# Two-layer hybrid attention block: the first attention stage takes the projections of its own queries and gate among its heads

## The chip, the core and the metric

The kernel runs on one core of one Trainium2 chip. The metric is the device time of one execution in microseconds (us), median of several runs. One execution was taken by the hardware profiler; its busy times, waits and the time of every instruction are what the text below calls the profile or the trace. The engines are named as in the profile: PE (TensorE matmul) and PEld (its weight load), DVE (VectorE), ACT (ScalarE), POOL (GpSimd), and SP (SyncE), whose queue issues the DMAs. "L685" is line 685 of the kernel.

## What is computed

Two layers (DEPTH = 2) of a mixer block on 512 latent tokens and 256 context tokens of width 1024. All tokens share the weights of a layer. Per layer:

- a modulation vector of 3 x 1024 values from `silu(c) @ w_ada + b_ada`, once for the latent and once for the context tokens: shift, scale and gate;
- `h = rms_norm(x) * (1 + scale) + shift`, for both token sets;
- one projection `h @ w_in` to 3584 columns, split among three head groups. Group A is differential attention: 4 heads, each with two query and key parts of 32 dimensions and one value of 64, so that a head needs two softmaxes and subtracts `lambda` times the second from the first. Group B is grouped-query attention with 6 query heads and 2 key and value heads. Group C is neighbourhood attention with 6 heads and a relative-position bias. Groups A and B have rotary position factors; queries and keys are RMS-normalized per head;
- latent queries attend to their latent keys and all context keys in one softmax; context queries to context keys only, and these only in the first layer, since the output is the latent stream;
- each group's output is multiplied by `silu` of its gate columns, the three are concatenated, multiplied by `w_out` and added to the residual through the modulation gate.

## The kernel before

**Precision.** Matmuls that need fp32 accuracy are made of three: each operand is split into a high part and a low part (`whi`, `wlo` for weights; two `bigL` or `bigC` tiles for `h`), and high x high, high x low and low x high are summed (`mm3`, L682; its three matmuls are L685, L686 and L687). Probabilities, queries, keys and values are split in the same way into two fp16 parts.

**Token tiles.** Tokens come in six tiles of 128: j = 0 to 3 are latent, 4 and 5 context.

**Projection chunks.** The columns of `w_in` are cut into chunks of at most 384 columns (`CH`, L258). For group A these are `a0` (all keys and the values of heads 0 and 1), `a1` (the values of heads 2 and 3, and all queries) and `ga` (the gate, 256 columns). Group B has `b0`, `b1` and `gb`, group C `c0`, `c1`, `c2` and `gn`. `proj` (L715) makes one chunk, token tile by token tile: 24 matmuls into one of two PSUM tiles named `p`, in four steps, after each of which it yields (such a step is called a quantum here), then `evac` (L663). For queries and keys that is a copy and a square on ACT, a sum on DVE, rotary products mostly on POOL (`qk_turn`), a power -1/2 on POOL (`rsqrt`, L156), made for two token tiles at a time, then a product (L504), a cast and a subtraction, and a DMA transpose into place (L540). For gates it is `gate_evac` (L603): tanh on ACT, a product on DVE, for group A a product on POOL (L611), and a write to DRAM (`g_d`); the attention that needs the gate reads it back by `gate_load` (L970).

**Weights.** `WStream` (L53) loads the chunks' weights in pieces of 256 rows and splits each piece: high part by ACT (L82), low part by a subtraction (L85). Six split pieces are kept (`HLB`); each time a piece has served its last token tile, the next is split. The engine of the subtraction goes by the name of the current phase (`VSHARE`, L38): POOL in phases "A" and without a name, DVE in phases "1" and "C", both in turn in "B".

**Attention.** `attn` (L981) walks through units. For group A a unit is one head of one latent token tile (16 units), plus, in layer 0, one head of one context tile (8 units). Per unit of group A:

1. `stage_S`: the scores of the two parts, each into a PSUM tile of 768 columns (two such tiles exist);
2. `stage_M`: the maximum over the row on DVE (L836), the bias of the exponential on ACT (L838);
3. `stage_E`: the exponential on ACT (L850) into a `p32` tile; three of these exist, a unit uses two;
4. `stage_H`, one unit later: the two parts combined on DVE (L866), the fp16 high part on ACT (L870), the low part on POOL (L871), and a DMA transpose into `pt` (L873), of which four exist;
5. `stage_PV`, four units after the scores: the product with the values (L906, L907), and at each fourth unit `pv_evac` with the head norm and the gate (L912 to L935).

**The modulation's rest.** `ada_blocks` (L214) makes one block of 128 modulation columns per step: two loads of 256 KB into two `adw` tiles, 16 matmuls (L236), a copy on DVE (L241), two more matmuls (L243) and a small DVE instruction. `proj` calls it once in every `st["cad"]` token tiles. It takes its PSUM tile from the two named `pv` in phase "1" and from the two named `p` otherwise.

**Order.** The text below is traced into one list of instructions. A scheduler then plays that list through in a simulated time and writes down each engine's order: whatever is ready, the earliest written first. `prio(-400)` lets `stage_S` count as written 400 instructions earlier, `prio(-100)` the loads of a modulation step 100. Each engine then runs its own list strictly in that order, with semaphores between engines. `both` (L1060) writes the units of one group and the quanta of the chunks that fill in (`fill`, L1037) in turn, in proportion; its argument `lead` says how many quanta are written ahead of the first unit. Per layer the text is: chunk `a0` for all tiles (`proj_first`), the chunks of `F1`, attention A with the chunks of `FA`, attention B with those of `FB`, attention C with `FC`, and the output projection.

Of the kernel before, what the change touches and what calls it, by code (L numbers as in the profile page):

```python
# [33 lines left out]


REST = {"C": 7}
AK = [[6, 2, 0, 2], [0, 1, 0, 2]]
VSHARE = {"HA": (0, 1), "H": (0, 1), "G": (1, 1), "T": (1, 4), "HC": (1, 8), "WB": (1, 2), "WC": (1, 1),  # L38
          "W1": (1, 1)}

# [69 lines left out]
def tile_hybrid_block(ctx: ExitStack, tc: tile.TileContext, xT_d, cT_d, ng_d, w_ada, bT_d, w_in, w_out,  # L110
# [7 lines left out]
    V, A, G, PE, SP = nc.vector, nc.scalar, nc.gpsimd, nc.tensor, nc.sync  # L118

    share = Share(nc)  # L120
# [49 lines left out]
    st = {}  # L170
# [82 lines left out]
    def ada_step():  # L253
# [4 lines left out]
    CH = {  # L258
# [4 lines left out]
    }  # L263
    FA = ["b0", "b1", "gb"]
    FB = ["c0", "c1", "c2", "gn"]
    FC = ["y", "o"]
    YE = 2
    F1 = ["a1", "ga"]
    ORDER = [c for c in ["a0"] + F1 + FA + FB + FC if c in CH]
    VCOL = {"a0": (256, 384), "a1": (0, 128), "b0": (128, 256), "c1": (0, 384)}  # L270
    vn = {}

# [11 lines left out]
    for l in range(DEPTH):  # L284
        for c in ORDER:
            cols, n = CH[c]
# [328 lines left out]
    def open_y(l):  # L615
        for k in "hl":
            yT[k] = [big(0, F32R)] + ([big(1, F32R)] if l == 0 else [])
# [411 lines left out]
    def run(gen):  # L1029
        for _ in gen:  # L1030
            pass
# [5 lines left out]
    def fill(l, toks):  # L1037
        for c in toks:
            if c in CH:
                yield from proj(l, [c])  # L1040
            elif c == "y":
                n = 6 if l == 0 else 4
                for j in range(0, n, 2):
                    y_pair(l, j)
                    yield
                    yield
                for j in range(n):
                    if (l, "B", j) not in turned:
                        y_build(l, "gb", j)
                    yield  # L1050
            elif c == "n":
                for db in range(KT):
                    while any((l, "C", j) not in turned for j in range(3)):
                        yield
                    out_head(l, db)
                    yield
            else:
                yield from out_parts(l)

    def both(l, g, chunks, lead=0):  # L1060
        share.phase = g
        f = fill(l, chunks)
        nf = n_quanta(l, chunks)
        na = len(units(l, g)) + 4
        for _ in range(lead):
            next(f, None)
        done = [lead]

        def pump():
            next(f)  # L1070
            done[0] += 1

        st["pump"] = pump
        for x, _ in enumerate(attn(l, g)):
            want = min(nf, lead + (nf - lead - REST.get(g, 0)) * (x + 1) // (na - (YE if g == "B" else 0)))
            while done[0] < want:
                next(f, None)
                done[0] += 1
            if g == "B" and done[0] >= nf and st.get("y") != l:
                run(f)  # L1080
                open_y(l)
                st["y"] = l
        run(f)
# [115 lines left out]
    if True:  # L1199
# [47 lines left out]
        proj_first(0, "a0", [[0, 1, 2, 3, 4, 5]], before0)  # L1247
        for _ in range(AK[0][0] + 1):
            ada_step()
        for l in range(DEPTH):  # L1250
            share.phase = "1"
            st["cad"] = AK[l][1]
            run(fill(l, F1))
            st["cad"] = AK[l][2]
            both(l, "A", FA)
            st["cad"] = AK[l][3]
            both(l, "B", FB)
            while st["done"] < (24 if l == 0 else 32):
                ada_step()
            st["cad"] = 0  # L1260
            both(l, "C", FC + ["n"] * (l + 1 == DEPTH))
            if l + 1 == DEPTH:
                out_tail(l)
                break
            x = [big(0), big(1)]
            open_norm()
            rs = [None, None]
            for db in range(KT):
                out_final(l, db, 1, x[1])
            rs[1] = norm_finish(1)  # L1270
            for db in range(KT):
                out_final(l, db, 0, x[0])
            hT[1] = (big(1, F32R), big(1, F32R))
            for kt in range(KT):
                prio(-800)(build_h)(l + 1, 1, kt, x[1], rs[1])

            def before1(gi, kt):
                if gi == 1:
                    if kt == 0:
                        rs[0] = norm_finish(0)  # L1280
                        hT[0] = (big(0, F32R), big(0, F32R))
                    prio(-800)(build_h)(1, 0, kt, x[0], rs[0])

            proj_first(1, "a0", [[4, 5], [0, 1, 2, 3]], before1)
# [77 lines left out]
```

## Time and profile before

| | |
|---|---|
| median of 3 runs | 934.97 us (934.93 to 936.88) |
| the profiled execution | 930.04 us, span 928.2 us |
| mean granted TensorE clock over the span | 0.95 |
| first score matmul of group A, layer 0 and layer 1 | 107.55 us and 602.99 us from the span's start |
| first gate of `ga` multiplied on POOL (L611), layer 0 | 116.5 us |

The times inside the kernel count from the span's start. In the tables of the trace a row of a group holds the line, engine, operation, output and inputs, shape and count, then the busy time in us and the mean duration in ns, then the idle time of the engine just before these instructions and what ended it. A row of a wait says who waited for whom, us in total, how often, and the longest. A row in order of time begins with start and duration in us. A wait for several semaphores is put down to the one that came last.

### The profile page before, as it was taken

To read this page: it belongs to the slowest core of one execution; us is meant where nothing else is said; L and a number is where in the kernel's file an instruction comes from. 1 tells how busy PE (TensorE), PEld (TensorE's weight loads), DVE (VectorE), ACT (ScalarE), POOL (GpSimd) and SP (SyncE) were. 2 spreads that over 40 slices of the span, in tenths; PEclk is the share of its full clock that TensorE was granted. 3 is DMA by queue.
4 is the path that set the end of the run, shared out by engine and by line. 5 is a ranking of instruction groups with operands and counts; after the bars stand their busy time and mean duration, and the time that the engine had idled before them with its cause. 6 is when DMAs were issued, how large, how long until landed. Compare 5 with 4: busy or idle time off the path is not lost.

```text
span 928.2 us, 17966 instructions
## 1 busy us (share of the span) xinstructions
PE 829.5 (89%) x6386; PEld 709.7 (76%) x6386; DVE 682.7 (74%) x1306; ACT 592.3 (64%) x1269; POOL 541.3 (58%) x502
## 2 busy tenths in 40 slices
PE   5899997997998999797999989989959999988978
PEld 3788886786887889685777889878849888866757
DVE  5975788988678866467765797789877975855853
ACT  5334577885887687476563445478758978757740
POOL 2638846998798465432441047939988776732420
PEclk9899999998999999899999999999979999987979
DMA  9925895644979997989898713884556889995642
GB/s 307 331 90 135 204 215 133 154 85 127 194 156 221 195 221 170 227 213 229 183 234 235 243 61 101 184 189 101 140 132 156 168 188 249 240 253 134 134 114 83
DMA packets 361449, 165.47 MB, mean 178 GB/s; under 512 B 256656, under 2 KB 355216, under 8 KB 361104
## 3 DMA queue, kind: packets, MB, share of 16 engines
q1 hardware_dynamic: 361360, 164.33, 73.9%
q8 instruction: 50, 0.82, 0.4%
q14 instruction: 39, 0.32, 0.1%
HBM read 86.55 MB, written 15.47 MB: 110 GB/s over the span
## 4 chain that ended last, share of the span: by engine, by line
PE 46%; DVE 15%; DMA 13%; POOL 9%; issue 8%; ACT 7%; SPq 1%; DVEq 0%; POOLq 0%; ACTq 0%
PE proj L685 7%; PE proj L687 7%; PE proj L686 6%; PE sc L781 5%; DMA pt<-hl 4%; PE pv L906 3%; PE op L1093 3%; PE op L1094 3%; PE op L1095 2%; ACT p L850 2%; DVE mx L836 2%; DMA raw<-in_w_in_dram 2%; DMA stB<-in_btab_dram 2%; POOL hl L871 2%; POOL wlo L85 1%
## 5 line engine op out<-in xcount | busy, mean ns | idle before, releaser
L871 POOL TENSOR_TENSOR hl<-p,hl 128x768 f16<-128x768 f32 (+3 forms) x138 | 204.2, 1484 | 179.7 <-ACT hl L870 139.7
L685 PE MATMUL proj<-whi,bigL 128*128 128x384 f32 (+1 forms) x592 | 203.4, 344 | 9.8 <-DVE tb L608 3.8
L686 PE MATMUL proj<-wlo,bigL 128*128 128x384 f32 (+1 forms) x592 | 200.3, 338 | 0.9 <-POOL wlo L85 0.7
L687 PE MATMUL proj<-whi,bigL 128*128 128x384 f32 (+1 forms) x592 | 197.7, 336 | 0.0
L850 ACT ACTIVATE p<-sc,nb,gsc 128x768 f32<-128x768 f32 (+3 forms) x200 | 166.0, 844 | 14.3 <-DVE p L866 5.0
L836 DVE TENSOR_REDUCE mx<-sc 128x1 f32<-128x768 f32 (+2 forms) x128 | 118.7, 931 | 31.7 <-PE sc L781 31.2
L685 PEld LDWEIGHTS proj<-whi,bigL 128*128 128x128 f32 x592 | 115.4, 195 | 19.9 <-DVE tb L608 5.4
L870 ACT CAST hl<-p 128x768 f16<-128x768 f32 (+3 forms) x144 | 103.7, 725 | 33.0 <-DMA pt<-hl 18.5
L686 PEld LDWEIGHTS proj<-wlo,bigL 128*128 128x128 f32 x592 | 115.5, 195 | 3.9 <-POOL wlo L85 1.6
L687 PEld LDWEIGHTS proj<-whi,bigL 128*128 128x128 f32 x592 | 114.4, 194 | 3.3 <-issue 2.4
L85 POOL TENSOR_TENSOR wlo<-raw,whi 128x768 fp32r<-128x768 f32 (+1 forms) x44 | 82.9, 1893 | 30.0 <-ACT whi L82 24.8
L82 ACT CAST whi<-raw 128x768 fp32r<-128x768 f32 (+1 forms) x104 | 80.3, 779 | 30.8 <-DMA raw<-in_w_in_dram 16.2
L906 PEld LDWEIGHTS <-pt 128*128 128x128 f16 x736 | 65.9, 99 | 41.2 <-DMA pt<-hl 25.7
L85 DVE TENSOR_TENSOR wlo<-raw,whi 128x768 fp32r<-128x768 f32 (+1 forms) x60 | 65.2, 1090 | 25.3 <-ACT whi L82 22.5
L685 PE MATMUL proj<-whi,bigC 128*128 128x384 f32 (+2 forms) x224 | 75.8, 339 | 0.8 <-ACT xn L468 0.8
L686 PE MATMUL proj<-wlo,bigC 128*128 128x384 f32 (+2 forms) x224 | 74.8, 334 | 0.0
L687 PE MATMUL proj<-whi,bigC 128*128 128x384 f32 (+2 forms) x224 | 74.6, 335 | 0.0
L156 POOL TENSOR_TENSOR rsqb<-rsqb,half 128x12 f32<-128x12 f32 (+2 forms) x25 | 68.2, 2726 | 10.5 <-DVE rsqb L155 8.4
L907 PEld LDWEIGHTS <-pt 128*128 128x128 f16 x736 | 66.6, 100 | 4.2 <-issue 1.2
L906 PE MATMUL pv<-vA,pt 128*128 128x128 f16 (+2 forms) x424 | 52.2, 229 | 13.6 <-DMA pt<-hl 13.0
L838 ACT ACTIVATE nb<-mx,lnp,gsc 128x1 f32<-128x1 f32 (+1 forms) x104 | 39.6, 385 | 37.6 <-DVE mx L836 26.5
L781 PE MATMUL sc<-bigL 128*128 128x512 f16 (+4 forms) x184 | 46.1, 310 | 17.3 <-ACT p L850 16.7
(320 smaller groups left out, 2042.2 us busy)
## 6 DMA issues: line engine op xcount, KB each, us to landing
raw<-in_w_in_dram SPq DMA_DIRECT2D x56, 384.0 KB, 4.1
adw<-in_w_ada_dram SPq DMA_DIRECT2D x68, 256.0 KB, 3.8
raw<-in_w_in_dram SPq DMA_DIRECT2D x24, 256.0 KB, 3.6
raw<-in_w_out_dram SPq DMA_DIRECT2D x16, 384.0 KB, 4.0
g_d<-tb SPq DMA_DIRECT2D x20, 192.0 KB, 2.6
gt<-g_d SPq DMA_DIRECT2D x18, 192.0 KB, 2.9
hl<-in_w_ada_dram SPq DMA_DIRECT2D x12, 256.0 KB, 5.0
pt<-in_w_ada_dram SPq DMA_DIRECT2D x12, 256.0 KB, 5.2
```

The lines of the kernel that those rows point to most:

```text
L82: self.nc.scalar.copy(out=hi, in_=raw2)
L85: self.share("W").tensor_tensor(out=lo, in0=raw2, in1=hi.bitcast(F32), op=ALU.subtract)
L156: G.tensor_tensor(out=y, in0=x, in1=half[:, 0:n], op=ALU.pow)
L685: PE.matmul(ps, lhsT=xh, rhs=hi, start=(kt == 0), stop=False)
L686: PE.matmul(ps, lhsT=xh, rhs=lo, start=False, stop=False)
L687: PE.matmul(ps, lhsT=xl, rhs=hi, start=False, stop=(kt == KT - 1))
L781: PE.matmul(ps, lhsT=q, rhs=k, start=n == 0, stop=n == b[2] - 1)
L836: V.tensor_reduce(out=mx[:, 0:ns], in_=ps[:, 0:w * ns].rearrange("p (a b) -> p a b", b=w), axis=AX.X, op=ALU.max)
L850: A.activation(out=p[:, w * x:w * x + w], in_=u["ps", i][:, w * x:w * x + w], func=AF.Exp, bias=u["nb", i][:, x:x + 1], scale=lc[l]["sc"][ ...
L870: A.copy(out=hl[:, 0:n], in_=p)
L871: lo_eng.tensor_tensor(out=hl[:, n:2 * n], in0=p, in1=hl[:, 0:n], op=ALU.subtract)
L906: PE.matmul(po[r, :], lhsT=pt[:, b, r], rhs=V_[:, vt, c0:129], start=first, stop=False)
```

## The change

`F1` is gone: `a1` and `ga` are now the first two chunks of `FA`, so they are written among the units of attention A, not ahead of them. `both` is called for group A with `lead` = 9: nine quanta, which is two finished token tiles of `a1` and the beginning of the third, are written ahead of the first unit. After unit x the text has reached 9 + (n - 9)(x + 1) / m quanta, rounded down, with n = 120 and m = 28 in layer 0 and n = 96 and m = 20 in layer 1. The order in which weights are loaded (`ORDER`) stays what it was.

Phase "1" is no longer set inside the loop over the layers; it now holds only from the first `proj_first` to the first attention A. The first attention A and the chunks in it all run under the name "A", with what hangs on the name: the engine of the weights' low part and the PSUM tile of the modulation steps.

The cadence of modulation steps (`AK`) has three numbers a layer now. The first, 6, is as before. In layer 0 there is one step per 5 token tiles over the 30 tiles of attention A (before: one per 2 over the 12 tiles of `F1`, none in attention A). In layer 1 there is one per 2 over 24 tiles (before: one per tile over the 10 tiles of `F1`, none in attention A). Stage B keeps one per 2.

```diff
-AK = [[6, 2, 0, 2], [0, 1, 0, 2]]
+AK = [[6, 5, 2], [0, 2, 2]]
...
-    FA = ["b0", "b1", "gb"]
+    FA = ["a1", "ga", "b0", "b1", "gb"]
     FB = ["c0", "c1", "c2", "gn"]
     FC = ["y", "o"]
     YE = 2
-    F1 = ["a1", "ga"]
-    ORDER = [c for c in ["a0"] + F1 + FA + FB + FC if c in CH]
+    LEAD = {"A": 9}
+    ORDER = [c for c in ["a0"] + FA + FB + FC if c in CH]
...
         for l in range(DEPTH):
-            share.phase = "1"
             st["cad"] = AK[l][1]
-            run(fill(l, F1))
+            both(l, "A", FA, LEAD["A"])
             st["cad"] = AK[l][2]
-            both(l, "A", FA)
-            st["cad"] = AK[l][3]
             both(l, "B", FB)
```

## Prediction

> **What bounds the kernel now.** I read the head of the page first, then the busy time by stretch, then the waits of PE inside those stretches, then the instructions around the first scores.
>
> ```profile
> span 928.2 us, 17966 instructions
> PE 829.5 (89%) x6386; PEld 709.7 (76%) x6386; DVE 682.7 (74%) x1306; ACT 592.3 (64%) x1269; POOL 541.3 (58%) x502
> ```
>
> The profiled execution took 930.04 us with a span of 928.2 us; the median of the timed runs, 934.97 us, lies 4.93 us above it. PE is idle for 928.2 - 829.5 = 98.7 us in all, so no reordering is worth more than that, and the change touches only the two first attention stages. The busy times by stretch show these (columns: stretch, its length, busy time and instructions of PE, PEld, DVE, ACT and POOL, granted clock, DMA share, GB/s). The first three rows are layer 0: projections alone, then attention A early and late. The last three are layer 1, in the same order.
>
> ```profile
> 70.00:107.00 37.00, 35.66 (x264) 30.64 (x264) 22.44 (x62) 15.97 (x41) 32.93 (x34) 0.95 0.63 141
> 107.00:150.00 43.00, 36.90 (x344) 30.66 (x345) 36.13 (x71) 32.58 (x82) 20.03 (x18) 0.96 0.97 228
> 150.00:226.00 76.00, 65.51 (x450) 58.56 (x448) 67.61 (x93) 55.20 (x131) 72.84 (x73) 0.93 0.53 119
> 570.00:603.00 33.00, 32.25 (x292) 29.43 (x290) 23.35 (x60) 16.21 (x41) 31.61 (x33) 1.00 0.76 177
> 603.00:630.00 27.00, 23.22 (x197) 20.09 (x198) 22.38 (x48) 21.57 (x55) 11.79 (x17) 1.00 0.80 182
> 630.00:695.00 65.00, 51.47 (x359) 44.81 (x356) 56.51 (x78) 46.53 (x109) 60.49 (x57) 0.89 0.53 124
> ```
>
> Three things are to be seen. Before the first scores (70 to 107, 570 to 603) PE is 96 to 98% busy and POOL 89 to 96%. In the first part of attention (107 to 150, 603 to 630) no engine is full: DVE is highest in layer 0 with 36.13/43 = 84%, PE in layer 1 with 86%, and POOL is below half. After that POOL is nearly full: 72.84/76 = 96% in layer 0, 60.49/65 = 93% in layer 1, while PE loses 10.5 and 13.5 us. So the stage first leaves POOL empty and is later bound by it.
>
> What PE waits for in the early part (first two rows: 108 to 160; next three: 598 to 640) and in the full part of layer 1 (last two: 640 to 695):
>
> ```profile
> PE sc L781 <- ACT p L850: 4.9, 4, 2.6
> PE ada L236 <- DMA adw<-in_w_ada_dram: 1.4, 2, 0.9
> ...
> PE sc L781 <- ACT p L850: 2.2, 2, 1.5
> PE ada L236 <- DMA adw<-in_w_ada_dram: 1.2, 2, 1.0
> ...
> PE sc L781 <- ACT p L850: 6.3, 3, 3.9
> PE pv L906 <- DMA pt<-hl: 4.9, 3, 3.1
> ```
>
> A score waits until the exponential has read its PSUM tile, and that sits at the end of maximum (DVE), exponential (ACT) and subtraction (POOL): only three `p32` tiles exist and a unit uses two. PE is held up by this ring of engines, not by lack of matmuls.
>
> **Part 1, the head start of two query tiles.** The new text lets attention begin after 9 quanta, two projected query tiles, where the old one puts 12 tiles (layer 1: 10) ahead of it. But the written order is only a priority, and scores already carry a lead of 400 places. The first scores stand here: first row of the DMA issues, then the turned context keys, the turned first query tile, DVE's weight splits and PE's projection at that moment, and the first score of layer 0 and of layer 1.
>
> ```profile
> DMA to landing us min/median/max: 3.1/3.8/6.2
> 97.99 5.11 SPq L540 DMA_TRANSPOSE bigC<-stg  x2
> 103.78 1.23 SPq L540 DMA_TRANSPOSE bigL<-stg  x1
> 103.34 2.06 DVE L85 TENSOR_TENSOR wlo<-raw,whi 128x512 fp32r<-128x512 f32 x2
> 105.45 1.10 DVE L85 TENSOR_TENSOR wlo<-raw,whi 128x512 fp32r<-128x512 f32 x1
> 107.13 0.28 PE L685 MATMUL proj<-whi,bigL 128*128 128x256 f32 x1
> 107.55 0.39 PE L781 MATMUL sc<-bigL 128*128 128x512 f16 x1
> 602.99 0.39 PE L781 MATMUL sc<-bigL 128*128 128x512 f16 x1 [0.41 <-DMA bigL<-stg]
> ```
>
> 103.78 plus a landing of 3.8 is 107.58, so the score of layer 0 ran as soon as its query had landed, and layer 1 waited 0.41 us for the same transfer. Neither waited for the ten later tiles. What lies ahead of those transposes (rotary and power steps of `a0` on the 89% busy POOL) is written before the changed place in both texts, and until then PE has nothing but `a1` and `ga` to project. I take 0. At best the three DVE splits that stand at 103.34 to 106.55 and now leave DVE let it come 3.2 us sooner; a loss would need a longer chain ahead of it, which the new text does not write.
>
> **Part 2, the order after the first scores.** The projection at 107.13 is 256 wide, so the six `a1` tiles are through and `ga` has begun: some 7 of the 12 tiles, 28 quanta, in the new text too. Now comes the difference: in the old text all gate tiles stand ahead of every maximum, exponential and subtraction of attention; in the new one 9 + 111(x + 1)/28 quanta stand ahead of what follows unit x, 28 for x = 4, so the units 0 to 4 stand ahead of the tiles still open, which fill in behind. No instruction is added. The attention units can run further ahead while POOL is empty, and then POOL has less left when it is full. What that is worth I bound by POOL's own work, at the rate that it reached when full (0.958 in layer 0, 0.931 in layer 1), with the splits of part 3 added (11.65 and 12.9 us):
>
> - layer 0, 107 to 226: (20.03 + 72.84 + 11.65) / 0.958 = 109.1 us where it took 119: 9.9 us.
> - layer 1, 603 to 695: (11.79 + 60.49 + 12.9) / 0.931 = 91.5 us where it took 92: 0.5 us.
>
> PE does not forbid it: 36.90 + 65.51 = 102.4 us of its 119. So the bounds are 0 and -10.4 us. I take half, **-5.2 us**: the ring of three `p32` tiles keeps units from running freely ahead, and the waits for it (4.9 and 2.2 us in the early part) are of the size of that half.
>
> **Part 3, eight weight splits a layer.** The phase name decides who subtracts: DVE in phase "1", POOL in phase "A". Six weight pieces are kept ready, so the last tile of `a1` frees four places (last two pieces of `ga`, first two of `b0`) and that of `ga` four more (last two of `b0`, first two of `b1`): 6 pieces of 512 columns and 2 of 768. Layer 0, then layer 1 (in whose seven DVE splits one of `a0`'s time is counted too):
>
> ```profile
> L85 DVE TENSOR_TENSOR wlo<-raw,whi 128x512 fp32r<-128x512 f32 x6 | 6.5, 1092 | 0.6 <-ACT wlo L278 0.6
> L85 DVE TENSOR_TENSOR wlo<-raw,whi 128x768 fp32r<-128x768 f32 x2 | 1.9, 952 | 0.8 <-ACT whi L82 0.8
> L85 POOL TENSOR_TENSOR wlo<-raw,whi 128x768 fp32r<-128x768 f32 x12 | 23.1, 1942 | 5.1 <-ACT wlo L278 2.8 <-ACT whi L82 2.3
> L85 DVE TENSOR_TENSOR wlo<-raw,whi 128x512 fp32r<-128x512 f32 x7 | 5.0, 716 | 0.9 <-ACT whi L82 0.5 <-ACT wlo L278 0.5
> L85 DVE TENSOR_TENSOR wlo<-raw,whi 128x768 fp32r<-128x768 f32 x2 | 2.8, 1394 | 0.0
> L85 POOL TENSOR_TENSOR wlo<-raw,whi 128x768 fp32r<-128x768 f32 x10 | 21.4, 2152 | 1.2 <-ACT whi L82 1.2
> ```
>
> DVE gets rid of 8.4 us and of 6 x 0.716 + 2.8 = 7.1 us. POOL has no 512-wide split here; two thirds of the wide one gives 6 x 1.29 + 2 x 1.94 = 11.65 us and 6 x 1.43 + 2 x 2.15 = 12.9 us. They are already inside the sums of part 2, so **0** here. What hides them is POOL's idle time of 43.0 - 20.0 = 23.0 and 27.0 - 11.8 = 15.2 us right after the first scores; without that cover they cost their full 24.5 us, and the matmuls that need `wlo` are late next. But who holds up whom is also to be seen:
>
> ```profile
> 156.54 1.65 POOL L871 TENSOR_TENSOR hl<-p,hl 128x768 f16<-128x768 f32 x1
> 156.90 1.45 DVE L504 TENSOR_TENSOR xn<-xn,rsq 128x128 f32<-128x128 f32 x1
> 158.37 1.63 POOL L871 TENSOR_TENSOR hl<-p,hl 128x768 f16<-128x768 f32 x1
> 158.53 1.62 DVE L504 TENSOR_TENSOR xn<-xn,rsq 128x128 f32<-128x128 f32 x1
> ```
>
> A DVE product of 128 columns takes 1.45 and 1.62 us and ends about when POOL's subtraction ends, though it started after it. So a microsecond moved to POOL can come back as a blocked microsecond on DVE: at worst 24.5 - 15.5 = 9.0 us. I keep that as a rival. [...]
>
> **Part 4, the modulation steps.** Old cadence 2 in the first projections, none in attention A; new cadence 5 (layer 0) and 2 (layer 1) over all of the stage. The number of steps until stage B is the same, 6 in layer 0; in layer 1 the list runs out in both. But outside phase "1" a step takes its PSUM tile from the two that the projections use: its first matmul may wait for one on PE, with scores and projections queued behind, and the next projection waits while the step holds it. Where that is already so, in the stage with attention B, and where the moved ones stand now (16 matmuls a step: 7, 6 and 7 steps):
>
> ```profile
> L236 PE MATMUL ada<-adw,cS x112: 272/273/298, 266.4 to 360.8; 128*32 128x128 f32 x112
> L236 PE MATMUL ada<-adw,cS x96: 269/273/298, 108.9 to 254.6; 128*32 128x128 f32 x96
> L236 PE MATMUL ada<-adw,cS x112: 272/273/298, 572.4 to 609.2; 128*32 128x128 f32 x112
> PE proj L685 <- DVE gnk L322: 2.0, 1, 2.0
> PE ada L243 <- DVE vnc L545: 1.5, 1, 1.5
> ```
>
> The last two rows are all the waits of PE in 262 to 365 that a missing PSUM tile can explain: 3.5 us for 7 steps, 0.5 us each. 13 moved steps make 6.5 us without cover and nothing where scores stand ready; I take half, **+3.25**. Their loads, two of 256 KB a step on SP's queue, move with them and no longer arrive late: the waits for `adw` above, 1.4 + 1.2, go: **-2.6**. Gate writes and gate loads move along on the same queue; a gate is needed first at the fourth unit's end, and its tile is projected before the scores begin, so 0.
>
> **Sum.** -5.2 + 0 + 3.25 - 2.6 = -4.55 us: the profiled execution would go from 930.04 to 925.5, the median from 934.97 to **930.4 us**.
>
> **Rivals.**
> - *It changes nothing.* Part 1 says that the stage was interleaved already. Against it: the priority of the units among the gate tiles does change. 935.0.
> - *Attention runs fully ahead.* All of part 2, the late loads gone, the steps covered: -10.4 - 2.6 = -13.0, so 922.0. Against it speaks the ring of three `p32` tiles.
> - *POOL is full (slower).* In layer 1 POOL has (31.61 + 11.79 + 60.49) of 125 us, 83%, and from 630 on it is the bound. If the eight splits land behind 630, all 12.9 us lie on the path; layer 0, with 23 us of cover, stays at 0: 947.9. It decides as soon as POOL's idle time after the first score of layer 1 falls below 12.9 of its 15.2 us.
> - *POOL's splits hold DVE (slower).* The 9.0 us of part 3 on an 84 to 89% busy DVE: 944.0. For it: the four rows. Against it: maxima, DVE's largest group, read PSUM and are not held.
> - *The two PSUM tiles (slower).* Part 2 brings nothing, and 6.5 us stand uncovered against 2.6 saved: 938.9.
>
> **Chances.** Forecast 0.36, own range 926 to 933; fully ahead 0.12; nothing 0.15; POOL full 0.17; DVE held 0.08; PSUM tiles 0.12. A measurement here can tell about 0.2%, 1.9 us, from no change. Faster is 0.36 + 0.12 = 0.48, same 0.15, slower 0.37. The range from 919 to 948 takes in all cases with their spread and leaves out less than 2 in 10 at its ends.
>
> **What would show it.** Part 1: the first scores within 3 us of 107.5 and, by the same distance, of 603. Part 2: POOL's busy time between the first score and 43 us later rises well above 20.0 us, more than the moved splits make, and the subtractions of attention come at shorter distance there. Part 3: eight splits a layer change from DVE to POOL; wrong if PE waits for `wlo` or if DVE's two-input operations get longer. Part 4: waits of a projection that begin while a modulation step holds a tile. The forecast fails if POOL is the bound from the first score on, or if attention A of layer 1 (92 us from 603 to 695) lengthens.

## The result, and the profile after

The changed kernel takes **944.23 us** (median of 8 runs, 939.18 to 948.27) where the kernel before took 934.95 us beside it (8 runs, 931.68 to 938.5): a ratio of **1.0098, 95% interval 1.007 to 1.0126**. It is 1% slower. The forecast was 930.4 us.

The profiled execution of the changed kernel took 948.27 us, 4 above its median; that of the kernel before lay 5 below. Their spans therefore differ by 18.3 us where the medians differ by 9.3. What a view shows of the difference is a matter of its kind and place, not of the last microsecond.

The head of the page of the changed kernel:

```profile
span 946.5 us, 17940 instructions
...
PE 833.4 (88%) x6386; PEld 718.2 (76%) x6386; DVE 671.2 (71%) x1290; ACT 591.0 (62%) x1269; POOL 568.9 (60%) x518
```

PE is idle for 946.5 - 833.4 = 113.1 us where it was idle for 98.7: 14.4 of the 18.3 us. PE itself is busy 3.9 us longer, with the same 6386 matmuls. DVE's work fell by 11.5 us and POOL's rose by 27.6 us.

The busy times by stretch of the changed kernel, in the columns of the prediction: from the first score of layer 0 on, and from that of layer 1 on, early and late.

```profile
111.50:155.00 43.50, 37.58 (x321) 34.29 (x324) 30.82 (x56) 32.38 (x83) 29.42 (x27) 0.92 0.75 173
155.00:230.00 75.00, 65.60 (x478) 57.76 (x471) 64.92 (x100) 54.03 (x130) 71.75 (x69) 0.95 0.58 136
...
603.50:630.00 26.50, 22.36 (x182) 19.19 (x183) 18.44 (x33) 19.44 (x49) 20.63 (x19) 0.87 0.82 179
630.00:695.00 65.00, 52.95 (x417) 47.23 (x416) 48.26 (x86) 45.55 (x111) 48.56 (x55) 0.89 0.59 137
```

POOL does more in the stretch that it left empty before (29.42 us after the first score of layer 0, where it was 20.03; 20.63 in layer 1, where it was 11.79). But this is not attention running ahead. The same stretches for the subtractions of attention alone (L871; columns: stretch, length, busy time and instructions of DVE and POOL, clock, DMA share, GB/s), two rows of the kernel before and two of the changed one, and then for the weight splits alone (L85) in the changed kernel:

```profile
107.00:150.00 43.00, 0.00 (x0) 7.38 (x5) 0.96 0.97 228
603.00:630.00 27.00, 0.00 (x0) 4.97 (x3) 1.00 0.80 182
...
111.50:155.00 43.50, 0.00 (x0) 8.31 (x5) 0.92 0.75 173
603.50:630.00 26.50, 0.00 (x0) 3.29 (x2) 0.87 0.82 179
```

```profile
111.50:155.00 43.50, 0.00 (x0) 8.72 (x6) 0.92 0.75 173
603.50:630.00 26.50, 0.00 (x0) 9.12 (x7) 0.87 0.82 179
```

The number of subtractions stays at five in layer 0 and falls from three to two in layer 1. The moved splits are what fills POOL there. Afterwards POOL is as full as before in layer 0 (71.75 of 75 us) and no longer full in layer 1 (48.56 of 65 us, where it was 60.49). Yet PE loses 12 us of those 65, about as much as before (13.5): there POOL is not the bound any more, and PE stands as long as it did.

What it stands for is told by the waits of PE over the whole span (who waited for whom, us in total, times, longest). First the kernel before, then the changed one:

```profile
PE sc L781 <- ACT p L850: 18.9, 16, 3.9
PE pv L906 <- DMA pt<-hl: 18.8, 19, 3.1
...
PE ada L236 <- DMA adw<-in_w_ada_dram: 4.8, 6, 2.0
...
PE ada L243 <- DVE adt L241: 2.1, 2, 1.7
```

```profile
PE sc L781 <- ACT p L850: 19.2, 17, 3.1
PE pv L906 <- DMA pt<-hl: 15.7, 16, 2.7
PE proj L685 <- DVE mG L249: 9.6, 5, 3.2
...
PE ada L243 <- DVE adt L241: 5.9, 8, 1.8
...
PE ada L236 <- DMA adw<-in_w_ada_dram: 2.8, 2, 2.1
...
PE ada L236 <- DVE vA L592: 2.5, 1, 2.5
...
PE proj L685 <- DVE mA L246: 1.7, 2, 0.9
```

`L246` and `L249` are the last DVE instruction of a modulation step: when it is done, the step gives its PSUM tile back. A projection that waits for it waits for a tile named `p`. These waits and those inside a step (L243) make 9.6 + 5.9 + 1.7 = 17.2 us, where they made 2.1. That is 15.1 us more. A step also waits for a tile itself, until DVE or ACT has read a projection out of it: 2.5 us above, 1.3 for L468 and 0.9 for L608, 4.7 us where there was none. The waits for the ring of attention (`p`, `pt`) are only 2.8 us smaller, and those for late loads 2.0.

These waits belong to the list: `e10_lead17` below has nearly the same list for PE, and in its profiled execution, whose span is 10.3 us shorter, they make 7.8 + 6.0 + 1.9 = 15.7 us in place of the 17.2. But they are not the loss one for one. Of the 14.4 us that PE idles longer, 4.0 lie ahead of the first score of layer 0 (19.7 us, where it was 15.7), where next to none of these waits stands.

One of these waits as it happens, right after the first scores of layer 0: PE in order of time (start, duration), then DVE in the same microseconds.

```profile
103.24 0.43 PE L236 MATMUL ada<-adw,cS 128*32 128x128 f32 x8 [0.70 <-DMA adw<-in_w_ada_dram]
...
110.36 0.42 PE L236 MATMUL ada<-adw,cS 128*32 128x128 f32 x8
...
112.17 0.28 PE L243 MATMUL ada<-sel,adt 128*128 128x2 f32 x2
115.45 0.39 PE L685 MATMUL proj<-whi,bigL 128*128 128x256 f32 x1 [3.00 <-DVE mG L249]
```

```profile
111.52 1.76 DVE L512 TENSOR_TENSOR stg<-xn,stg 128x512 f16<-128x512 f32 x1 [0.38 <-ACT stg L511]
113.20 0.94 DVE L836 TENSOR_REDUCE mx<-sc 128x1 f32<-128x768 f32 x1
...
114.33 0.94 DVE L836 TENSOR_REDUCE mx<-sc 128x1 f32<-128x768 f32 x1
115.19 0.20 DVE L249 TENSOR_SCALAR mG<-ada,bT 128x2 f32<-128x2 f32 x1
```

And POOL beside the first of these:

```profile
111.46 1.27 POOL L85 TENSOR_TENSOR wlo<-raw,whi 128x512 fp32r<-128x512 f32 x1
```

The step takes its tile with its first eight products at 103.24 and has the second eight at 110.36 and the last two at 112.17, 0.43 + 0.42 + 0.28 = 1.13 us of PE time. It keeps the tile until 115.39, 12.15 us. Its last instruction, 0.20 us long, stands in DVE's list behind the subtraction that makes the low part of queries and two score maxima. That subtraction takes 1.76 us here, where one of the same shape at 102.77 took 0.89, with two POOL products of 0.46 and 0.90 us beside it; here a moved weight split of 1.27 us runs on POOL beside it, so part 3 may have a share in this wait, though one row does not show it. All that while one of the two projection tiles is gone, and PE, with the next projection first in its list, ends by doing nothing for 3.00 us. Paired in this way, the 20 steps up to attention B of the two layers hold a tile for 6.5 us each on average in the changed kernel (the first six of them still one named `pv`). In the kernel before it is 7.1 us, leaving aside one step of 29.8 us that begins at 543.50, while layer 0 ends.

### The profile page after: what moved, and what is told of

Read it like the earlier page. It is cut to its first block, busy times and chain, and to the rows that moved or that the text cites. A ratio compares the mean times of both kernels' runs of the same rounds, so it can differ in the third digit from the quotient of the medians.

```text
span 946.5 us, 17940 instructions
## 1 busy us (share of the span) xinstructions
PE 833.4 (88%) x6386; PEld 718.2 (76%) x6386; DVE 671.2 (71%) x1290; ACT 591.0 (62%) x1269; POOL 568.9 (60%) x518
## 5 line engine op out<-in xcount | busy, mean ns | idle before, releaser
L871 POOL TENSOR_TENSOR hl<-p,hl 128x768 f16<-128x768 f32 (+3 forms) x138 | 209.5, 1522 | 173.4 <-ACT hl L870 155.2
L685 PE MATMUL proj<-whi,bigL 128*128 128x384 f32 (+1 forms) x592 | 208.9, 353 | 22.4 <-DVE mG L249 8.8
L686 PE MATMUL proj<-wlo,bigL 128*128 128x384 f32 (+1 forms) x592 | 203.5, 344 | 1.8 <-DVE wlo L85 1.2
L687 PE MATMUL proj<-whi,bigL 128*128 128x384 f32 (+1 forms) x592 | 202.6, 344 | 0.0
L836 DVE TENSOR_REDUCE mx<-sc 128x1 f32<-128x768 f32 (+2 forms) x128 | 119.2, 932 | 38.9 <-PE sc L781 35.9
L685 PEld LDWEIGHTS proj<-whi,bigL 128*128 128x128 f32 x592 | 119.7, 202 | 32.2 <-DVE mG L249 9.6
L85 POOL TENSOR_TENSOR wlo<-raw,whi 128x768 fp32r<-128x768 f32 (+1 forms) x60 | 104.5, 1747 | 38.6 <-ACT whi L82 33.4
L686 PEld LDWEIGHTS proj<-wlo,bigL 128*128 128x128 f32 x592 | 119.9, 203 | 4.3 <-DVE wlo L85 1.5
L687 PEld LDWEIGHTS proj<-whi,bigL 128*128 128x128 f32 x592 | 119.1, 202 | 3.0 <-issue 1.0
L82 ACT CAST whi<-raw 128x768 fp32r<-128x768 f32 (+1 forms) x104 | 80.2, 778 | 37.7 <-DMA raw<-in_w_in_dram 17.1
L906 PEld LDWEIGHTS <-pt 128*128 128x128 f16 x736 | 65.7, 99 | 35.2 <-DMA pt<-hl 20.5
L838 ACT ACTIVATE nb<-mx,lnp,gsc 128x1 f32<-128x1 f32 (+1 forms) x104 | 39.5, 384 | 26.1 <-DVE mx L836 19.7
L85 DVE TENSOR_TENSOR wlo<-raw,whi 128x768 fp32r<-128x768 f32 (+1 forms) x44 | 47.6, 1086 | 11.0 <-ACT whi L82 10.2
```

Source lines behind the costliest of these rows:

```text
L82: self.nc.scalar.copy(out=hi, in_=raw2)
L85: self.share("W").tensor_tensor(out=lo, in0=raw2, in1=hi.bitcast(F32), op=ALU.subtract)
L685: PE.matmul(ps, lhsT=xh, rhs=hi, start=(kt == 0), stop=False)
L686: PE.matmul(ps, lhsT=xh, rhs=lo, start=False, stop=False)
L687: PE.matmul(ps, lhsT=xl, rhs=hi, start=False, stop=(kt == KT - 1))
L836: V.tensor_reduce(out=mx[:, 0:ns], in_=ps[:, 0:w * ns].rearrange("p (a b) -> p a b", b=w), axis=AX.X, op=ALU.max)
```

## The experiments

Each ratio is to the kernel before on the same chip, with its 95% interval. "Order" is the new text of the stage, "splits" the eight weight splits a layer on POOL, "steps" the modulation steps with their cadence and PSUM tile.

### One part of the change undone

`e1_ada_psv`: the changed kernel, with the steps of attention A in the tiles named `pv`.

```diff
-ps = (psV if share.phase == "1" else psP).tile(..., tag="pv" if share.phase == "1" else "p", ...)
+ps = (psV if share.phase in ("1", "A") else psP).tile(..., tag="pv" if share.phase in ("1", "A") else "p", ...)
```

> The changed kernel, but the modulation steps inside attention A take their PSUM tile from the two named pv again. Theory PSUM (a modulation step holds one of the two tiles of the projections; the waits of PE for it and around it sum to about 16 us in the changed kernel's trace): most of the loss goes, ratio to the kernel before 0.998 to 1.004, and the waits of a projection for the step's last DVE instruction (L249, L246) disappear. Theory splits (eight weight splits a layer on POOL) and theory order (attention written ahead of the projections costs by itself): 1.007 to 1.012.

Measured 937.82 us, 1.0024 (0.9997 to 1.0052), as the theory of the tile had it: its trace has only 0.5 + 1.1 us of the waits that made 17.2. `e2_splits_dve`: the changed kernel, with the eight splits a layer back on DVE.

```diff
-self.share("W").tensor_tensor(out=lo, ...)
+eng = self.nc.vector if i in self.vset else self.share("W")
+eng.tensor_tensor(out=lo, ...)
...
+W.vset = {i for l in range(DEPTH) for i in pidx[l, "ga"][2:] + pidx[l, "b0"] + pidx[l, "b1"][:2]}
```

> The changed kernel, but the eight weight splits a layer that went to POOL are on DVE again, named piece by piece; the modulation steps stay as changed. Theory splits: ratio to the kernel before 0.998 to 1.003. Theories PSUM and order: 1.006 to 1.012, the 16 us of waits around the modulation steps still there.

Measured 957.05 us, 1.0232 (1.0186 to 1.0278): without the move to POOL the changed kernel is 1.3% slower still, which no theory had. `e3_order_only`: the new order alone, with the splits on DVE as in e2, the tiles as in e1, and the steps where they were (one per 2 tiles of `a1` and `ga` in layer 0, one per tile in layer 1).

```diff
-AK = [[6, 5, 2], [0, 2, 2]]
+AK = [[6, 0, 2], [0, 0, 2]]
...
-if st["cad"] and st["n"] % st["cad"] == 0:
+cad = (2, 1)[l] if c in ("a1", "ga") else st["cad"]
+if cad and st["n"] % cad == 0:
```

> The changed order of the text alone: a1 and ga among the units after nine quanta, but the modulation steps as before (one per two tiles of a1 and ga, one per tile in layer 1, PSUM tiles named pv) and the eight splits on DVE. Theory order: ratio to the kernel before 1.007 or more. Theories PSUM and splits: 0.993 to 1.002, below 1 by as much as the order itself is worth (the forecast's part 2 was 5.2 us, 0.6%).

Measured 940.48 us, 1.0053 (1.0021 to 1.0085): the order alone loses half a per cent, between the ranges of the theories. `e6_lead25` and `e10_lead17`: the changed kernel with another head start.

```diff
-LEAD = {"A": 9}
+LEAD = {"A": 25}
```

> The changed kernel with a lead of 25 quanta instead of 9: the whole of a1 is written ahead of the first unit, ga and the rest among the units. Theory order: the loss shrinks to half or less, ratio to the kernel before 1.000 to 1.005. Theories PSUM and splits: unchanged, 1.007 to 1.012, since the steps still fall into attention A and take the projections' tiles and the splits stay on POOL.

> The changed kernel with a lead of 17 quanta, four query tiles instead of two. The planner gives almost the same orders as with 9 (14 lines of PE's 7575 differ). Theory lead (how many tiles are written ahead matters): below 1.007. Theory that the written lead is ignored because the first scores wait for keys and query anyway: 1.007 to 1.013, as the changed kernel.

Measured 946.06 us, 1.0116 (1.0064 to 1.0169), and 943.35 us, 1.0075 (1.0042 to 1.0108). Both intervals overlap that of the change. With 17 the scheduler writes nearly the list of 9 for PE (14 lines of difference among 7575), so that run shows mostly that the result repeats. The head start is not what costs.

### One part alone on the kernel before

`e4_before_ada`: no step in the first projections, one per 3 (layer 0) and 2 (layer 1) tiles in attention A, in the tiles `p`.

```diff
-AK = [[6, 2, 0, 2], [0, 1, 0, 2]]
+AK = [[6, 0, 3, 2], [0, 0, 2, 2]]
```

> The kernel before with part 4 alone: no modulation step in the first projections; in attention A one per 3 tiles (layer 0, 6 steps) and one per 2 (layer 1, 7 steps), which then take one of the two PSUM tiles of the projections. Order and splits as before. Theory PSUM (with the pv tiles the changed kernel fell from 1.0098 to 1.0024): 1.004 to 1.010. Theory that the modulation steps cost only in the new order: 0.998 to 1.002.

Measured **921.59 us, 0.9851 (0.982 to 0.9882)**: it beats both kernels, and neither theory had that. `e5_before_splits`: the eight splits a layer on POOL (the edit of e2 with GpSimd for VectorE).

> The kernel before with part 3 alone: the eight weight splits a layer after a1 and ga are made by POOL, all else as before. By the forecast's rival of a full POOL: 1.005 to 1.014. By the second experiment (in the changed kernel the same splits on DVE made it 1.3% slower): no loss, 0.992 to 1.002, and if below 0.998 a version faster than both.

Measured 948.45 us, 1.0138 (1.0109 to 1.0166). `e8_before_psp`: the steps of the first projections keep their place, but take a tile `p`.

```diff
-ps = (psV if share.phase == "1" else psP).tile(...)
+pool_, tag_ = (psV, "pv") if st["done"] <= 6 else (psP, "p")
+ps = pool_.tile([128, 512], F32, tag=tag_, name="ada")
```

> The kernel before, order, cadence and splits untouched; only the PSUM tile of the modulation steps in the first projections changes from pv to p. Theory PSUM in its strict form (the tile alone, wherever the step stands): 1.004 to 1.010, with waits of a projection for the step's last DVE instruction. If it needs attention beside it (DVE busy with maxima, so that the step holds its tile longer): 0.999 to 1.003.

Measured 950.95 us, 1.0164 (1.0139 to 1.0189), more than the strict form of the theory allowed. `e9_order_pool`: the new order with the splits on POOL, the steps as before in place and tile (e3 without the edit of e2). This is the change without part 4.

> The changed order with the modulation steps as before (among a1 and ga, PSUM tiles pv) and the eight splits on POOL as in the changed kernel. Against the third experiment (the same with the splits on DVE, 1.0053) it prices the splits; against the first (1.0024, the steps spread, pv) the cadence. Theory PSUM with splits on POOL harmless: 0.995 to 1.003. Theory order (the written order costs by itself): 1.004 or more.

Measured **930.23 us, 0.9938 (0.9915 to 0.9961)**. Parts 1 to 3 together gain 0.6%, and what turns the change into a loss is the modulation steps: 1.0098 - 0.9938 = 1.6%, some 15 us. `e11_late_steps`: as e9, but no step in `a1` and `ga` and then the cadence and tiles of e4.

> The changed order and the splits on POOL, with the modulation steps placed as in the fourth experiment: none while a1 and ga are projected, then one per 3 tiles (layer 0) and one per 2 (layer 1), PSUM tiles p. Theory PSUM: 1.005 or more, as the changed kernel, since the steps take the projections' tiles. Theory place (what matters is that no step falls between the first tiles, where keys and queries are made ready): 0.982 to 0.995. Theory plan scatter (each new plan moves by about 1% either way, whatever part is changed): anything from 0.985 to 1.016, no help.

Measured 957.44 us, 1.0223 (1.0176 to 1.027). The same placing that gained 1.5% in the old order is 2.2% slower than before in the new one.

So single parts do not add up. The splits on POOL cost 1.4% in the old order (e5) and gain 1.15% (e9 against e3) and 1.3% (the change against e2) in the new one. The new order loses 0.5% with the splits on DVE (e3) and gains 2.0% with them on POOL (e9 against e5).

### Do parts have a price at all?

Every edit makes the scheduler write the whole list anew, so I changed the list without changing any work: the lead of the scores 300 instead of 400.

```diff
-@prio(-400)
+@prio(-300)
```

> The kernel before with one number of the planner changed: scores count as written 300 instructions earlier instead of 400. No work, engine, tile or step changes, but the planned orders do (6342 lines of PE's). Theory plan scatter: off 1 by 0.4% or more, either way. Theories that explain the times by parts (PSUM, splits, order): 0.997 to 1.003.

> The changed kernel with the same number at 300. Theory plan scatter: off 1.0098 by 0.4% or more, either way. Theories by parts: 1.007 to 1.013.

Measured 941.65 us, 1.0054 (1.0026 to 1.0082), for the kernel before and 947.18 us, 1.0096 (1.0062 to 1.0129), for the changed one. An edit without work moves the first by 0.5% and leaves the second where it was. I then repeated four variants with this lead.

> The kernel before with the modulation steps of the first projections moved into attention A (fastest so far, 0.985 of the kernel before), and the scores' lead in the planner set from 400 to 300. Theory of parts (the moved steps save time by themselves): 1.0054 (the kernel before at 300) less the same 1.5%, so 0.990 +- 0.003, about 927 us. Theory of the redrawn plan (what a part is worth depends on the whole order): the saving differs by at least 0.5% from 1.5%, so below 0.985 or above 0.9955.

> The changed kernel with the modulation steps of attention A in the tiles named pv, and the scores' lead at 300. Theory of parts (the two projection tiles cost the changed kernel 0.7%): 0.7% below the changed kernel at 300 (1.0096), so 1.002 +- 0.003, about 938 us. Theory of the redrawn plan: a difference other than 0.7% by 0.5% or more, so below 0.9975 or above 1.0075.

> The changed kernel's order and its splits on POOL with the modulation steps as before (0.994 at 400), and the scores' lead at 300. Theory of parts: the modulation's part costs the changed kernel the same 1.6% at 300, so 1.0096 - 0.016 = 0.994 +- 0.003, about 930 us. Theory of the redrawn plan: off by 0.5% or more from that, below 0.989 or above 0.999.

> The kernel before with the eight splits a layer on POOL (1.0138 at 400), and the scores' lead at 300. Theory of parts: 1.0054 + 0.0138 = 1.019 +- 0.003, about 954 us. Theory of the redrawn plan: off by 0.5% or more from that, most likely below 1.014.

e14 (e4 with 300): 921.51 us, 0.9852 (0.9813 to 0.9891). Here the scheduler wrote the very same list as with 400, so it is a second measurement of e4 and tells the theories not apart. e15 (e1 with 300): 948.44 us, 1.0141 (1.0103 to 1.018), not 1.002: the gain from the tiles `pv` has become a loss. e16 (e9 with 300): 923.79 us, 0.9877 (0.9832 to 0.9921): part 4 costs 1.0096 - 0.9877 = 2.2% here, some 20 us. e17 (e5 with 300): 948.14 us, 1.0127 (1.0088 to 1.0165), 0.7% above e12 and not 1.4%. With the changed lead these lists part from the others only in attention B of layer 0, so the two leads are not two independent draws.

Part 4 has two halves, the place of the steps and their tile. Two last runs fill the square: the edit of `e9_order_pool` with the tiles `p` of the change, at both leads.

> The changed kernel with the modulation steps where they were before (one per 2 tiles of a1 and ga in layer 0, one per tile in layer 1, none else in attention A), in the tiles named p as in the change. It fills the fourth place of a square: steps as before in pv 0.994, spread in pv 1.002, spread in p 1.010. Theory of the place (spreading the steps over the stage is what costs): as with pv, 0.994 to 0.998, about 932 us. Theory of the tile (the two projection tiles are what costs): at least 0.7% above the pv version, 1.001 or more, about 938 us or more.

> The same with the scores' lead in the planner at 300. The other three places of the square there: steps as before in pv 0.988, spread in pv 1.014, spread in p 1.010. Theory of the place: 0.985 to 0.995, about 927 us. Theory of the tile: 1.000 or more. If the two leads disagree on which theory holds, neither place nor tile has a price of its own.

Measured 963.86 us, 1.0288 (1.0253 to 1.0323), and 959.15 us, 1.0269 (1.0225 to 1.0312).

| steps, lead | tiles `pv` | tiles `p` |
|---|---|---|
| as before, 400 | 0.9938 (e9) | 1.0288 (e18) |
| spread over attention A, 400 | 1.0024 (e1) | 1.0098 (the change) |
| as before, 300 | 0.9877 (e16) | 1.0269 (e19) |
| spread over attention A, 300 | 1.0141 (e15) | 1.0096 (e13) |

Neither half has one price. For steps that stand close together beside the projections the tiles `p` cost 3.5 and 3.9%, and 1.6% in the old order (e8). For spread steps the tiles make +0.7 and -0.45%. Spreading costs 0.9 and 2.6% in `pv` and saves 1.9 and 1.7% in `p`. Nor do the waits of PE around the steps decide by themselves: e13 has 9.2 + 4.2 + 1.6 us of those that made 17.2 in the change, e15 only 2.9 + 0.4, and e15 is not the faster one. The change leaves the one corner that is fast at both leads.

The heads of the pages of e9 and e18, in this order:

```profile
span 928.6 us, 17958 instructions
...
PE 825.8 (89%) x6386; PEld 708.8 (76%) x6386; DVE 652.6 (70%) x1290; ACT 589.6 (63%) x1269; POOL 565.9 (61%) x518
```

```profile
span 962.2 us, 17933 instructions
...
PE 838.9 (87%) x6386; PEld 716.9 (75%) x6386; DVE 676.3 (70%) x1290; ACT 588.9 (61%) x1269; POOL 560.6 (58%) x518
```

PE's idle time is 102.8 and 123.3 us. e18 against e9 differs only in the tile of the steps: 33.6 us of span, of which 20.5 are idle and 13.1 are matmuls that took longer. Projections wait only 2.9 + 0.4 us for a step's tile in e18. The larger waits stand inside the steps, for their DVE copy and their loads, and were 0.4 and 2.3 us in e9:

```profile
PE ada L243 <- DVE adt L241: 11.3, 10, 3.6
PE ada L236 <- DMA adw<-in_w_ada_dram: 10.8, 9, 2.2
```

So the tile's high price here is measured, but the held tile is not shown to be the way in which it is paid.

Where the change loses 3.00 us, e9 has two steps under way beside the first scores. PE in order of time:

```profile
104.28 0.42 PE L236 MATMUL ada<-adw,cS 128*32 128x128 f32 x8
...
108.19 0.43 PE L236 MATMUL ada<-adw,cS 128*32 128x128 f32 x8
...
109.33 0.39 PE L781 MATMUL sc<-bigL 128*128 128x512 f16 x1 [0.27 <-DMA bigL<-stg]
...
110.38 0.43 PE L236 MATMUL ada<-adw,cS 128*32 128x128 f32 x8 [0.23 <-DMA adw<-in_w_ada_dram]
...
112.28 0.36 PE L687 MATMUL proj<-whi,bigL 128*128 128x256 f32 x1
```

The first step, too, lasts from 104.28 until its last DVE instruction ends at 113.55, 9.3 us, and the second begins meanwhile. But they hold tiles `pv`, which nobody else wants before the first product with the values (129.3 us), and the projections run on behind them.

Last, the waits of PE in e4 and in e9:

```profile
PE pv L906 <- DMA pt<-hl: 10.7, 13, 2.5
PE sc L781 <- ACT p L850: 10.5, 8, 4.1
...
PE ada L243 <- DVE adt L241: 6.2, 5, 2.3
...
PE proj L685 <- DVE mG L249: 4.9, 4, 2.4
...
PE proj L685 <- DVE mB L249: 2.2, 1, 2.2
```

```profile
PE sc L781 <- ACT p L850: 31.2, 19, 4.0
PE pv L906 <- DMA pt<-hl: 18.9, 19, 2.1
```

e4 has waits of the change's kind, 6.2 + 4.9 + 2.2 = 13.3 us. But its waits for the ring fell from 18.9 + 18.8 = 37.7 to 21.2 us, by more than that. In the change the ring gave back 2.8 us for 15.1. In e9 no row of a projection or a step that waits in this way is longer than 0.6 us, and the ring's waits are the largest of the four kernels. A wait of PE for one thing often takes the place of a wait for another; what an edit costs is the balance, and the list of a single kind does not show it.

## Why the prediction was wrong, point by point

**The step that failed is part 4 of the sum**, "+3.25" for the PSUM tiles and "-2.6" for the loads, +0.65 us together. The runs put 1.6% in its place, some 15 us (the change against e9), and 2.2%, some 20 us, at the other lead. The loads did come in time (4.8 to 2.8 us of waiting, 2.0 of the 2.6). The price of a step was mis-sized. I took it, 0.5 us, from the stage with attention B, where seven steps cost 3.5 us, and halved it. A step holds its tile 6.5 us for 1.1 us of work, since its DVE instructions, and at times its second load, stand in strict lists behind others. The waits for steps and inside them are 15.1 us longer than before in place of at most 6.5, and steps wait 4.7 us more for a tile. The time a step holds its tile could be read in the trace of before (7.1 us); I priced the wait by another stage and did not ask for it. Rival "the two PSUM tiles" named this mechanism and the side, at 938.9 us; its bound of 6.5 us was too small by more than half. That part 4 makes the loss is shown by e9 and e16; that these waits are the way in which it does is argued, since e15 is rid of them and no faster than e13.

**Part 2 and the sum of parts 1 to 3.** The forecast was -5.2 us. e9 is these three parts and measured 930.23 against 935.94 us beside it, -5.7 (0.9938). That the sum came out is luck. At the other lead the same parts make -12.5 us (e16, 923.79 against 936.32). The mechanism of part 2 did not appear: by its own mark POOL's busy time should have risen by more than the moved splits make, and the splits make 8.72 of the 9.4 us in layer 0 and all of the 8.8 us in layer 1, with no more subtractions of attention than before; e9 too has five and three of them in the 43 and 27 us after its first scores. Rival "attention runs fully ahead" falls with that. Nor did the terms hold: part 3 was priced at 0 and alone costs 1.4% (e5), part 2 alone costs 0.5% (e3). They are worth something only together. Their prices were read from one schedule, as if it stayed when the next part was added.

**Part 1.** The first score of layer 1 came at 603.51, within 3 us of the forecast. In layer 0 it came at 111.51, 4.0 late, which by my own mark counts against me. But e13, whose lists are the same up to attention B, has it at 107.70. Between 71.8 and 78.6 us the changed kernel's clock was 0.50 and e13's 1.00 (columns as above; the changed kernel first):

```profile
71.80:78.60 6.80, 6.12 (x25) 5.74 (x26) 3.36 (x9) 3.32 (x11) 6.80 (x8) 0.50 0.36 110
```

```profile
71.80:78.60 6.80, 6.80 (x58) 6.00 (x51) 4.38 (x20) 2.42 (x8) 6.80 (x7) 1.00 0.37 112
```

So the delay belongs to this execution and not to the change; the head start is worth nothing, as forecast, and e6 and e10 agree (first scores at 110.48 and 108.93).

**Part 3.** The splits moved as said. L85 goes from 44 to 60 instructions on POOL, 82.9 to 104.5 us, and from 60 to 44 on DVE, 65.2 to 47.6 us. Sixteen splits changed engine: 21.6 us more on POOL (forecast 24.5), 17.6 less on DVE (forecast 15.5). The cover held: POOL was 29.42 of 43.5 us busy after the first score of layer 0. Rival "POOL is full" falls with the 48.56 of 65 us in layer 1, since seven of the eight splits of that layer ran ahead of 630 us, and with e2, which takes the load off POOL and is slower. In the old order e5 lost 1.4%, as this rival had it there; what it lost by is not examined. Rival "POOL's splits hold DVE" falls as a price of 9.0 us, though not as a mechanism. Of the twelve products of the shape that I had shown being held, those over 0.7 us, seven before and four after, each began while a POOL subtraction ran (L85 or L871) and ended about 0.15 us behind it; the others took 0.28 to 0.68 us. On average the twelve take 786 ns where they took 1160, and all products of L504 together take 60.5 us where they took 66.9; the subtractions of L512, one of which is the row of 1.76 us above, take 18.7 us where they took 16.5. In sum that is 79.2 us where it was 83.4, so in sum these operations were not held longer. The maxima of L836 were not held, as I had said: none of the 128 took more than 0.96 us in either kernel.

**My marks for failure.** "The forecast fails if attention A of layer 1 lengthens": from the first score to the first score of attention B it went from 120.7 to 131.4 us. Before, then after, in the columns of the stretches:

```profile
603.00:723.70 120.70, 102.69 (x746) 90.89 (x746) 101.15 (x156) 92.69 (x217) 95.72 (x94) 0.94 0.60 143
```

```profile
603.50:734.90 131.40, 108.48 (x796) 95.34 (x797) 95.93 (x154) 90.61 (x215) 104.38 (x102) 0.88 0.64 148
```

PE is busy 5.8 us longer in it, with 50 more matmuls and a mean clock of 0.88 instead of 0.94, and idle 4.9 us longer. The mark came true, but it proves less than I thought. The changed kernel comes to this stage with some 120 matmuls fewer behind it (4145 where it was 4265), so a part of the length is work that the kernel before had done by then; and e9, which is faster than the kernel before, takes 123.1 us for it.

**What stays open.** Why the same steps gain 1.5% in the old order (e4) and lose in the new one (e11) is told only as a balance of waits, not derived. The square rests on two leads that share the first third of the list. An edit without work moved single variants by -0.6% (e9 to e16) to +1.2% (e1 to e15), so differences below that, such as the 0.7% of e1 against the change, are not the price of anything. The 3.5 and 3.9% of the tile of dense steps lie well above that scatter. The 1.6 and 2.2% of part 4 lie above any single shift, but a difference holds two of them, so that it rests on both leads having the same sign.

## What to carry to other kernels

Before a step with a small PSUM need is moved, ask whose tile it takes and how long it holds it: not its PE time, but the time until its last reader has run on an engine with a strict list, and who wants that tile meanwhile. Where a scheduler writes the whole order anew, a change of several parts has no sum of prices: run the parts alone and together, and first measure what an edit without any work moves (here up to 1.2%). Two variants that came out of taking it apart are faster than both kernels: the old order with the steps moved into attention A (921.6 us), and the new order and splits with the steps left as they were (930.2 us, or 923.8 us at the other lead).

## What the runs showed of the hardware

I had read PE's idle time as the whole loss, and as the most that a reordering can win. But in e18 against e9 13.1 us of the 33.6 are busy time of the same 6386 matmuls. Behind many gaps PE runs at half clock for a while. The 3.00 us wait shown above is one of them; PE in order of time behind it, in the changed kernel:

```profile
115.80 0.28 PE L687 MATMUL proj<-whi,bigL 128*128 128x256 f32 x1
115.91 0.28 PE L685 MATMUL proj<-whi,bigL 128*128 128x256 f32 x1
...
117.15 0.41 PE L686 MATMUL proj<-wlo,bigL 128*128 128x256 f32 x1
117.36 0.41 PE L687 MATMUL proj<-whi,bigL 128*128 128x256 f32 x1
```

```profile
112.40:115.50 3.10, 0.10 (x2) 0.05 (x1) 3.10 (x6) 1.32 (x5) 2.15 (x3) 1.00 0.80 215
116.20:119.60 3.40, 3.40 (x18) 3.40 (x18) 1.53 (x4) 2.97 (x9) 2.89 (x4) 0.50 0.81 247
```

The 256-wide matmuls stand 0.11 to 0.12 us apart, then 0.21 for 3.4 us. From 116.15 to 119.68 the 17 distances from one matmul to the next take 3.53 us, where 0.12 each would make 2.0: the wait of 3.00 us cost about 1.5 us more. Over the 20 profiled executions of this case the clock stood at half for 73 us (e4, mean clock 0.960) to 129 us (e18, 0.933) of the span; it was 92.5 us in the kernel before and 99.8 in the changed one. In these two traces 33 of the 35 stretches at half clock last 3.41 us or a multiple of it, and the other two end with the record. A straight line through the 20 gives 1.07 us of span for each us of PE's idle time and 0.24 for each us at half clock (largest distance from the line 4.0 us); the two go up together, so the line does not tell them apart sharply. In the rows above the half clock begins at 116.2 us, 0.8 us after the wait of 3.00 us has ended, and lasts 3.41 us, with PE busy all the time. Divided into pieces of 3.41 us that begin and end where the clock changes, the 20 profiles have 260 pieces at full clock in which PE was busy for less than 45%, and every one was followed by half clock, while of the 4165 in which it was busy for 70% or more, 11 were; in the traces of the kernel before and the changed one alone it is 25 of 25, and 2 of 426. So in these traces more than 1.9 us of idle time within one such piece was enough each time.
